# One scan step for both directions of an RWKV-7 scan: a shared PSUM bank, joint copies, four opening products together

## The chip, the cores and the metric

The kernel runs on one core of one Trainium2 chip. The metric is the device time of one execution in microseconds (us), smaller is better. Engines are called PE (TensorE, matrix products), PEld (its weight loads), DVE (VectorE), ACT (ScalarE), POOL (GpSimd) and SP (SyncE, which here only issues DMAs). PSUM is the memory that PE writes its products into, in banks of 2 KB for each of 128 partitions; SBUF is the on-chip memory that everything else works from.

## The reference, cut to what matters

The kernel computes one layer of a diffusion backbone over 1024 latent tokens of 1024 channels, with 256 context tokens in front. Three parallel branches are fed by one input projection: a neighbourhood attention, an RWKV-7 time mixing that runs in both directions, and a gated spatial mixing. Each branch is projected and gated, the sum is projected once more, and a SwiGLU feed-forward follows. The change touches the RWKV branch alone, whose core is a recurrence on one 64x64 state for each of 8 heads and 2 directions:

```python
def delta_scan(state0, inputs, emit):
    def step(S, inp):
        r_t, w_t, k_t, v_t, kk_t, a_t = inp
        s_kk = jnp.einsum('...vk,...k->...v', S, kk_t)
        S = (S * w_t[..., None, :] - s_kk[..., :, None] * (kk_t * a_t)[..., None, :]
             + v_t[..., :, None] * k_t[..., None, :])
        return S, (jnp.einsum('...vk,...k->...v', S, r_t) if emit else None)
    return lax.scan(step, state0, inputs)
```

It runs first over the 256 context tokens without output, and from there over the 1024 latent tokens with output. The backward direction runs over reversed time. The outputs of both directions are added, normalised per head and gated.

## The kernel before, in words

Stages in order of time: input scaling and the projections that the scan needs, the scan, the attention with the scan's readout beside it, the mixer (branch and output projections), and the feed-forward. Most wide products are split into a high and a low half (`hh`, `hl` and `wh`, `wl`) and made as three products of 128x512 each (lines 222 to 224, whose results are called `d` in the profile).

**The scan** (`rwkv_run`, line 561) works on chunks of 64 tokens. Within a chunk the recurrence is a triangular system, so a chunk costs a few products and one state update. Heads come in pairs; a job `m` is one head pair `j` and one block `i` of 256 tokens, that is four chunks `u`, for both directions. `L` lists 20 jobs, in the order of two head pairs in turn; block 0 is the context. A job needs three things:
- `prep` (line 625), once for each direction: loads, decays `E`, the products of the chunk's vectors into PSUM tiles `gr` (line 662), and their masked copies into `KKe`, `KKo` (three sets of buffers, line 647), `BB` and `G`.
- `invert` (line 691), once for both directions: `G` goes through DRAM, DVE solves small blocks (lines 704 to 709), the result comes back through DRAM, and 64x64 products (line 725) build the inverse `X`.
- `step` (line 744), once for each direction and chunk, 160 times in all. Here is what a step does, as the prediction follows it. Its *opening products* (752) multiply state and values `rv` by `KKe` and `KKo` into `sc[lo]` and `sc[hi]`, the two heads of the pair on partitions 0 to 63 and 64 to 127. DVE and ACT copy this right side to `rb` (755, 756). Two products with `X` (758) give the solution, which ACT and DVE copy, negated, to `ub` (759, 760). Six *closing products* (764, 767; in context blocks 771, 773) give new state and output in the same bank. DVE and ACT scale the new state into `rv` of the next chunk (777, 778), and ACT copies the output to `y` (782, twice). Each `matmul` of the program is two records of the trace.

`sc` has two PSUM banks (`bufs=2`), so the two directions' steps take turns on them: the next step of a direction takes the bank that its last one used. The framework keeps two engines off one bank at a time: DVE reads its half, then ACT reads the other. `rb` and `ub` are rings of four tiles with zeros outside the written blocks.

**What sets the order.** The program is traced in the order of the Python code, and the framework's scheduler then fixes every engine's order when the kernel is built, by that order and by its own cost estimates. Work traced late can be put into time that it believes idle. That is how 28 projections that are needed only after the scan (`filling`, line 542: queries for the attention and branch gates; `fill(4)` and `fill(24)` in `build`, traced after scan and attention) come to stand on PE between the products of the scan. They are called *fillers* here: 48 products of 128x512 each.

**Around a step.** `values` (584) loads the values of job `m+2` into `rv` by eight DMAs at SP, in four tiles of four chunks each. `y` goes to DRAM from ACT's queue (618), one DMA for each direction. The readout loads it again, one direction at a time (944, 945), as 4 KB rows with a chunk's token on the partitions.

Of the kernel before, what the change touches and what calls it, by code (L numbers as in the profile page):

```python
# [17 lines left out]
P = 128  # L18
# [18 lines left out]
LEAD, LAG, AHEAD = 2, 2, 5  # L37
NPP, NPT = 4, 3
SIDE = 16
NWR, NHT, NHS, NO4, NO2 = 3, 8, 2, 6, 4  # L40

PV = {}
# [16 lines left out]
class Kern:  # L59
# [501 lines left out]
    def rwkv_run(self):  # L561
        nc, a, c, rp, s = self.nc, self.a, self.c, self.rp, self.s
# [19 lines left out]
        rvs, Js = {}, {}  # L582

        def values(m):
            j, i = L[m]
            rv = rvs[m] = [[self.T([P, 4, 64], f"rv{d}{h}", 3) for h in range(2)] for d in range(2)]
            for d in range(2):
                if i == 0:
                    nc.gpsimd.memset(rv[d][0][0:64, 3 * d, :], 0.0)
                    nc.gpsimd.memset(rv[d][1][64:128, 3 * d, :], 0.0)  # L590
                V = s["vtok"][j]
                n0 = self.start(d, i)
                for h in range(2):
                    nc.sync.dma_start(rv[d][h][64 * (1 - h):64 * (1 - h) + 64, 0:4, :],
                                      bass.AP(V.tensor, V.offset + 64 * h + n0 * P, [[P, 64], [P * 64, 4], [1, 64]]))

        def prepare(m):
            j, i = L[m]
            G = self.T([P, 2, 4, 64], "G", 2)
            Js[m] = [self.prep(m, j, d, i, G[:, d]) for d in range(2)]  # L600
            self.invert(Js[m])

        self.filler = self.filling()
# [4 lines left out]
        for m, (j, i) in enumerate(L):  # L608
            if m + 2 < len(L):
                values(m + 2)  # L610
            y = [self.T([P, 2, P], f"y{d}", 2) for d in range(2)] if i else [None, None]
            for u in range(4):
                for d in range(2):
                    self.step(Js[m][d], d, i, u, rvs[m][d], rvs[m + 2][d] if i < 4 else None, y[d])
            if i:
                for d in range(2):
                    c0 = 4 * (i - 1) if d == 0 else 16 - 4 * i
                    nc.scalar.dma_start(s["Y"][d][j][:, 64 * c0:64 * c0 + 256], y[d].rearrange("p c v -> p (c v)"))
# [6 lines left out]
    def prep(self, m, j, d, i, G):  # L625
# [10 lines left out]
        E = self.T([P, 4, 65], "E", 6)  # L636
        nc.gpsimd.memset(E[:, :, 0:1], 1.0)
        nc.scalar.activation(E[:, :, 1:65], units(R(li)), AF.Exp, scale=-C05)
        le = self.T([P, 256], "le", 2)
# [7 lines left out]
        KKe, KKo = self.sets[(m % 3) * 2 + d]  # L647
# [9 lines left out]
        prev = None  # L657
        for u in range(4):
            re = (KKe[0:64, u, :].rearrange("p (x t) -> p x t", t=64)[:, 0:3:2, :] if lat else KKe[0:64, u, 0:64])
            for o, x, y in ((go, BK[64:128, u, :], KKo[64:128, u, 0:W]), (ge, BK[0:64, u, :], re)):  # L660
                with self.tc.issue_after(prev.ins) if prev is not None else nullcontext():
                    prev = nc.tensor.matmul(o[:, u, 0:W], x, y, start=True, stop=True)
# [4 lines left out]
        BB = self.T([P, 4, P], "BB", 6)  # L667
# [18 lines left out]
        for o, t in ((BB[0:64, :, 0:64], tr[0:64, :, 0:64]), (KKe[64:128, :, 64:128], tr[64:128, :, 0:64]),  # L686
                     (BB[64:128, :, 64:128], tr[0:64, :, 64:128]), (KKo[0:64, :, 128:192], tr[64:128, :, 64:128])):
            nc.scalar.activation(o, t, AF.Copy)
        return dict(KKe=KKe, KKo=KKo, G=G, BB=BB, E=E, n0=n0, lat=lat)

    def invert(self, jobs):
        nc, c = self.nc, self.c
# [48 lines left out]
        for d, J in enumerate(jobs):  # L741
            J["X"] = X[:, 4 * d:4 * d + 4]

    def step(self, J, d, i, u, rv, rvn, y):
        nc = self.nc
        lat, KKe, KKo, BB, X, E = J["lat"], J["KKe"], J["KKo"], J["BB"], J["X"], J["E"]
        v, w = (u, u + 1) if d == 0 else (3 - u, 2 - u)
        sc = self.ps.tile([P, 512], F32, name="sc", tag="sc", bufs=2)
        lo, hi = slice(0, 64), slice(64, 128)
        kk = (KKe[:, u], KKo[:, u])  # L750
        for z, q in enumerate((lo, hi)):
            nc.tensor.matmul(sc[q, 0:64], kk[z][:, 0:64], rv[z][:, v, :], start=True, stop=True)
        self.un += 1
        rb, ub = self.rb[self.un % 4], self.ub[self.un % 4]
        nc.vector.tensor_copy(rb[0:64, 0:64], sc[0:64, 0:64])
        nc.scalar.activation(rb[64:128, 64:128], sc[64:128, 0:64], AF.Copy)
        for q in (lo, hi):
            nc.tensor.matmul(sc[q, 64:128], X[:, u, :], rb[:, q], start=True, stop=True)
        nc.scalar.activation(ub[0:64, 0:64], sc[0:64, 64:128], AF.Copy, scale=-1.0)
        nc.vector.tensor_scalar(ub[64:128, 64:128], sc[64:128, 64:128], -1.0, None, ALU.mult)  # L760
        if lat:
            for z in range(2):
                for h, q in enumerate((lo, hi)):
                    nc.tensor.matmul(sc[q, 128 + 64 * z:192 + 64 * z], kk[z][:, 64 + 64 * h:128 + 64 * h], rv[z][:, v, :],
                                     start=(z == 0), stop=False)
            for q in (lo, hi):
                nc.tensor.matmul(sc[q, 128:256], BB[:, u, q], ub, start=False, stop=True)
            so = 192
        else:
            for z, q in enumerate((lo, hi)):  # L770
                nc.tensor.matmul(sc[q, 128:192], kk[z][:, 64 + 64 * z:128 + 64 * z], rv[z][:, v, :], start=True, stop=False)
            for q in (lo, hi):
                nc.tensor.matmul(sc[q, 128:192], BB[:, u, q], ub[:, q], start=False, stop=True)
            so = 128
        if not (i == 4 and u == 3):
            dst = (rv[0][:, w, :], rv[1][:, w, :]) if u < 3 else (rvn[0][:, 3 * d, :], rvn[1][:, 3 * d, :])
            nc.vector.tensor_scalar(dst[0][0:64], sc[0:64, 128:192], E[0:64, u, 64:65], None, ALU.mult)  # L777
            nc.scalar.activation(dst[1][64:128], sc[64:128, so:so + 64], AF.Copy, scale=E[64:128, u, 64:65])  # L778
        if lat:
            q = slice(64 * (v % 2), 64 * (v % 2) + 64)  # L780
            for z, p0, c0 in ((0, 64, 128), (1, 0, 192)):
                nc.scalar.activation(y[q, v // 2, 64 * z:64 * z + 64], sc[p0:p0 + 64, c0:c0 + 64], AF.Copy)


    def A(self, shape, tag, bufs, dt=F32):
# [149 lines left out]
    def readout(self):  # L935
        nc, a, s, c = self.nc, self.a, self.s, self.c
        for j in range(4):
# [4 lines left out]
            Y = self.X([P, 16, 64], "A4", 6)  # L942
            Y2 = self.X([P, 16, 64], "A4", 6)
            for y, d in ((Y, 0), (Y2, 1)):
                nc.sync.dma_start(y.rearrange("p c v -> p (c v)"), s["Y"][d][j])
# [515 lines left out]
```

## Time and profile before

| what | value |
|---|---|
| median of 3 runs | 2424.2 us (2419.29 to 2430.45) |
| the profiled execution, its own time | 2425.41 us |
| its span, first to last instruction | 2423.6 us |
| mean granted clock of PE | 0.974 |
| scan, from the first solution products to the last step | about 568 to 1155 us |
| attention, with readout | about 1160 to 1440 us |
| a stretch of fillers alone | within 1440 to 1500 us |
| mixer and feed-forward | from about 1500 us |

A profile row of a group reads: line, engine, operation, output<-inputs, shapes, count, then the time that the group keeps its engine busy, the mean of one in ns, and the idle time of the engine just before it with what ended it. A row of the windows view reads: start and end, length, then for PE, PEld, DVE, ACT, POOL the busy time and the count of instructions, and last PE's granted clock, the DMA engines' busy share and GB/s. Restricted to a tile, it counts the instructions that write or read that tile alone. A row of the timeline is start, length, engine, line, operation and tiles; "x4" merges four neighbours. Lengths of PE's rows overlap, because products are pipelined: what one costs is the distance from its start to the next start.

### The profile page before, as it was taken

How to read it: one execution, taken by the hardware profiler on the slowest of the kernel's cores; microseconds unless marked ns; L12 is line 12 of the kernel's file. 1: busy time of each engine (PE TensorE's matmuls, PEld its weight loads, DVE VectorE, ACT ScalarE, POOL GpSimd, SP SyncE). 2: the span in 40 equal slices, each digit the busy share in tenths (PEclk: the TensorE clock that was granted, in tenths of full speed). 3: DMA queues.
4: the chain of work that ended last, by engine and by line, in shares of the span. 5: the costliest groups of instructions: out<-in, count | busy, mean ns of one | idle time of the engine just before them, and what ended most of it. 6: DMA issues, size and time to landing. Idle time of an engine off the chain costs nothing. (4 is left out here: it accounts for less than half of the span.)

```text
span 2423.6 us, 40691 instructions
## 1 busy us (share of the span) xinstructions
PE 2288.6 (94%) x15352; PEld 1799.6 (74%) x15352; DVE 1557.5 (64%) x3290; ACT 948.3 (39%) x1985; POOL 684.2 (28%) x718
## 2 busy tenths in 40 slices
PE   6899999999999999989999999999799999999997
PEld 4778888776666766666777778778588888887886
DVE  8885446347777788774377833777665555555835
ACT  4432424233455445444355532232533333333421
POOL 6221213441121122111221330232433333425402
PEclk9999999999999999999999999999899999999999
DMA  7676444554344344432666564555132222237541
GB/s 248 213 235 164 142 137 150 173 146 116 91 100 110 96 118 111 101 71 60 186 183 172 178 216 163 168 196 161 61 105 79 79 81 85 88 138 269 170 161 53
DMA packets 276121, 337.53 MB, mean 139 GB/s; under 512 B 123314, under 2 KB 194226, under 8 KB 275924
## 3 DMA queue, kind: packets, MB, share of 16 engines
q1 hardware_dynamic: 208804, 240.91, 33.5%
q10 hardware_dynamic: 54608, 51.40, 7.1%
q0 software_dynamic: 12512, 42.62, 4.8%
q8 instruction: 121, 1.98, 0.3%
q14 instruction: 76, 0.62, 0.1%
HBM read 248.85 MB, written 85.99 MB: 138 GB/s over the span
## 5 line engine op out<-in xcount | busy, mean ns | idle before, releaser
L222 PE MATMUL d<-hh,wh 128*128 128x512 f32 x1056 | 431.4, 408 | 1.2 <-ACT stg L539 1.2
L224 PE MATMUL d<-hh,wl 128*128 128x512 f32 x1056 | 432.2, 409 | 0.0
L223 PE MATMUL d<-hl,wh 128*128 128x512 f32 x1056 | 431.5, 409 | 0.0
L224 PEld LDWEIGHTS d<-hh,wl 128*128 128x128 f32 x1056 | 201.5, 191 | 47.3 <-issue 4.4
L222 PEld LDWEIGHTS d<-hh,wh 128*128 128x128 f32 x1056 | 201.7, 191 | 45.1 <-issue 3.6
L223 PEld LDWEIGHTS d<-hl,wh 128*128 128x128 f32 x1056 | 201.5, 191 | 43.5 <-issue 2.3
L214 DVE TENSOR_TENSOR wl<-wr,wh 128x1024 fp32r<-128x1024 f32 x51 | 65.0, 1274 | 185.2 <-ACT wh L210 136.8
L210 ACT ACTIVATE wh<-wr 128x1024 fp32r<-128x1024 f32 x79 | 83.6, 1058 | 205.4 <-PE d L223 157.7
L214 POOL TENSOR_TENSOR wl<-wr,wh 128x256 fp32r<-128x256 f32 x112 | 87.2, 807 | 245.8 <-ACT wh L210 192.2
L239 DVE TENSOR_TENSOR o<-wr,o 128x1024 fp32r<-128x1024 f32 (+1 forms) x64 | 93.8, 1467 | 19.7 <-ACT o L236 19.2
L1022 PE MATMUL d<-dl,ah 128*128 128x512 f32 x252 | 98.3, 390 | 2.5 <-DVE dl L239 2.5
L906 PE MATMUL pv<-pT,V 128*64 128x128 f32 (+2 forms) x640 | 95.6, 287 | 4.5 <-ACT pT L894 3.0
L236 ACT ACTIVATE o<-wr 128x1024 fp32r<-128x1024 f32 (+1 forms) x64 | 59.2, 926 | 101.4 <-PE d L223 74.4
L1023 PE MATMUL d<-dh,al 128*128 128x512 f32 x252 | 98.1, 389 | 0.0
L1021 PE MATMUL d<-dh,ah 128*128 128x512 f32 x252 | 98.0, 389 | 0.0
L239 DVE TENSOR_TENSOR al<-ar,ah 128x512 fp32r<-128x512 f32 x42 | 42.1, 1020 | 75.1 <-ACT ah L236 75.1
L1016 POOL TENSOR_TENSOR wl<-wr,wh 128x1024 fp32r<-128x1024 f32 x16 | 42.7, 2671 | 167.9 <-DVE wr L1014 123.3
L778 ACT ACTIVATE rv<-sc,E 64x64 f32<-64x64 f32 x152 | 46.6, 308 | 108.4 <-DVE rv L777 90.2
L906 PEld LDWEIGHTS pv<-pT,V 128*64 128x64 f32 (+2 forms) x640 | 69.4, 139 | 24.4 <-issue 13.8
L1249 POOL TENSOR_TENSOR act<-act 128x512 f32<-128x512 f32 x22 | 28.7, 1306 | 194.3 <-issue 160.1
L707 DVE TENSOR_TENSOR dtmp<-gz,DD 64x15 f32<-64x15 f32 (+2 forms) x300 | 72.2, 241 | 11.4 <-POOL DD L703 3.7
L709 DVE TENSOR_TENSOR DD<-DD,dtmp 64x15 f32<-64x15 f32 (+2 forms) x300 | 73.7, 246 | 5.5
(403 smaller groups left out, 6019.4 us busy)
## 6 DMA issues: line engine op xcount, KB each, us to landing
wr<-wgu SPq DMA_DIRECT2D x45, 512.0 KB
dr<-wdn SPq DMA_DIRECT2D x42, 512.0 KB
wa<-wada SPq DMA_DIRECT2D x32, 512.0 KB
wr<-win SPq DMA_DIRECT2D x31, 512.0 KB
wr<-win ACTq DMA_DIRECT2D x28, 512.0 KB
s_gt<-stg ACTq DMA_DIRECT2D x48, 256.0 KB
wr<-wbr SPq DMA_DIRECT2D x24, 512.0 KB
g<-s_gt SPq DMA_DIRECT2D x48, 256.0 KB
```

The lines of the kernel that those rows point to most:

```text
L210: nc.scalar.activation(hi[:, :n], raw[:, :n], AF.Copy)
L214: (lo_eng or self.lo_eng).tensor_tensor(lo[:, q], raw[:, q], hi[:, q].bitcast(F32), ALU.subtract)
L222: nc.tensor.matmul(ps, w, xh, start=first and k == 0, stop=False)
L223: nc.tensor.matmul(ps, w, xl, start=False, stop=False)
L224: self.last = nc.tensor.matmul(ps, lo[:, P * k:P * k + P], xh, start=False, stop=last and k == n - 1)
L239: (lo_eng or nc.vector).tensor_tensor(lo, src, hi.bitcast(F32), ALU.subtract)
L707: nc.vector.tensor_tensor(t, z[:, q, q + 1:16].unsqueeze(2).to_broadcast([64, n, w]), Dm[:, q, 0:w].unsqueeze(1).to_broadcast([64, n, w]), ...
L709: nc.vector.tensor_tensor(Dm[:, q + 1:16, 0:w], Dm[:, q + 1:16, 0:w], t, ALU.add)
L906: nc.tensor.matmul(o, V[0:k, vt, 64 * e:64 * e + 64], pt[0:k, i, :], start=(i == 0), stop=(i == len(cols) - 1))
L1021: nc.tensor.matmul(ps, xh, wh, start=first, stop=False)
L1022: nc.tensor.matmul(ps, xh, wl, start=False, stop=False)
L1023: nc.tensor.matmul(ps, xl, wh, start=False, stop=last)
```

## The change

`step` serves both directions at once, so there are 80 of them.
- One bank `sc` of [128, 2, 256] holds both directions; still two banks, now used in turn by consecutive joint steps.
- `rb` and `ub` hold both directions ([128, 2, 128], rings of three). DVE copies the right side of both directions for head `lo` in one instruction, ACT for head `hi`; the same for the solution. The new state of head `lo` is one DVE product with a broadcast `E`; that of head `hi` stays two ACT instructions, one for each direction. The output is two ACT copies in place of four.
- `rv`, `y` and `E` are joint tiles; chunk `u` of the forward direction sits at index `u`, of the backward one at `7 - u`.
- The opening products are issued backward direction first, and the other three are tied behind the first one in PE's order.
- `y` now has a head on each half of the partitions, for all eight chunks. The readout therefore loads each direction's output with four DMAs of 64 partitions and 64-element runs in place of one of whole rows.

The number and shape of the products is the same. The core of the diff:

```diff
+NRB = 3
...
-        for i in range(4):
+        for i in range(NRB):
             for n, l in (("rb", self.rb), ("ub", self.ub)):
-                t = rp.tile([P, P], F32, name=f"{n}{i}")
+                t = rp.tile([P, 2, P], F32, name=f"{n}{i}")
...
-            rv = rvs[m] = [[self.T([P, 4, 64], f"rv{d}{h}", 3) for h in range(2)] for d in range(2)]
+            rv = rvs[m] = [self.T([P, 8, 64], f"rv{h}", 3) for h in range(2)]
...
+            E = self.T([P, 2, 4, 65], "E", 3)
+            Js[m] = [self.prep(m, j, d, i, G[:, d], E[:, d]) for d in range(2)]
...
-            y = [self.T([P, 2, P], f"y{d}", 2) for d in range(2)] if i else [None, None]
+            y = self.T([P, 8, 64], "y", 2) if i else None
             for u in range(4):
-                for d in range(2):
-                    self.step(Js[m][d], d, i, u, rvs[m][d], rvs[m + 2][d] if i < 4 else None, y[d])
+                self.step(Js[m], Es[m], i, u, rvs[m], rvs[m + 2] if i < 4 else None, y)
...
-    def step(self, J, d, i, u, rv, rvn, y):
+    def step(self, J, E, i, u, rv, rvn, y):
+        lat = i > 0
+        at = (u, 7 - u)
+        two = lambda p, q: slice(p, q + 1, q - p)
+        sc = self.ps.tile([P, 2, 256], F32, name="sc", tag="sc", bufs=2)
         self.un += 1
+        rb, ub = self.rb[self.un % NRB], self.ub[self.un % NRB]
+        prev = None
+        for d in (1, 0):
+            for z, q in ((1, hi), (0, lo)):
+                with self.tc.issue_after(prev.ins) if prev is not None else nullcontext():
+                    x = nc.tensor.matmul(sc[q, d, 0:64], J[d]["kk"][z][:, u, 0:64], rv[z][:, at[d], :], start=True, stop=True)
+                prev = prev or x
+        nc.vector.tensor_copy(rb[lo, :, 0:64], sc[lo, :, 0:64])
+        nc.scalar.activation(rb[hi, :, 64:128], sc[hi, :, 0:64], AF.Copy)
+        for d in range(2):
+            for q in (lo, hi):
+                nc.tensor.matmul(sc[q, d, 64:128], J[d]["X"][:, u, :], rb[:, d, q], start=True, stop=True)
+        nc.scalar.activation(ub[lo, :, 0:64], sc[lo, :, 64:128], AF.Copy, scale=-1.0)
+        nc.vector.tensor_scalar(ub[hi, :, 64:128], sc[hi, :, 64:128], -1.0, None, ALU.mult)
+        for d in range(2):
             for z in range(2):
                 for h, q in enumerate((lo, hi)):
+                    if lat or z == h:
+                        c0 = 128 + 64 * z * lat
+                        nc.tensor.matmul(sc[q, d, c0:c0 + 64], J[d]["kk"][z][:, u, 64 + 64 * h:128 + 64 * h], rv[z][:, at[d], :],
+                                         start=(z == 0 or not lat), stop=False)
             for q in (lo, hi):
+                o, x = (sc[q, d, 128:256], ub[:, d, :]) if lat else (sc[q, d, 128:192], ub[:, d, q])
+                nc.tensor.matmul(o, J[d]["BB"][:, u, q], x, start=False, stop=True)
+        so = 192 if lat else 128
         if not (i == 4 and u == 3):
+            o, w = (rv, two(u + 1, 6 - u)) if u < 3 else (rvn, two(0, 7))
+            nc.vector.tensor_tensor(o[0][lo, w, :], sc[lo, :, 128:192], E[lo, :, u, 64:65].to_broadcast([64, 2, 64]), ALU.mult)
+            for d in range(2):
+                nc.scalar.activation(o[1][hi, (w.start, w.stop - 1)[d], :], sc[hi, d, so:so + 64], AF.Copy, scale=E[hi, d, u, 64:65])
         if lat:
+            w = two(*at)
+            nc.scalar.activation(y[hi, w, :], sc[hi, :, 128:192], AF.Copy)
+            nc.scalar.activation(y[lo, w, :], sc[lo, :, 192:256], AF.Copy)
...
             for y, d in ((Y, 0), (Y2, 1)):
-                nc.sync.dma_start(y.rearrange("p c v -> p (c v)"), s["Y"][d][j])
+                for q in range(2):
+                    for h in range(2):
+                        nc.sync.dma_start(y[64 * q:64 * q + 64, h:16:2, :], s["Y"][d][j][64 - 64 * h:128 - 64 * h].rearrange(
+                            "p (n q v) -> p q n v", q=2, v=64)[:, q])
```

The removed body of the old `step` is in the listing above.

More of the change, by code (lines that the diff above doesn't have):

```diff
@@ L581, in rwkv_run @@
         L = [(2 * g + j, i) for g in range(2) for i in range(5) for j in range(2)]
-        rvs, Js = {}, {}
+        rvs, Js, Es = {}, {}, {}
         def values(m):
             j, i = L[m]
-            rv = rvs[m] = [[self.T([P, 4, 64], f"rv{d}{h}", 3) for h in range(2)] for d in range(2)]
+            rv = rvs[m] = [self.T([P, 8, 64], f"rv{h}", 3) for h in range(2)]
+            if i == 0:
+                for h in range(2):
+                    nc.gpsimd.memset(rv[h][64 * h:64 * h + 64, 0:8:7, :], 0.0)
+            V = s["vtok"][j]
             for d in range(2):
[L588 to L591, printed above, removed]
                 n0 = self.start(d, i)
                 for h in range(2):
-                    nc.sync.dma_start(rv[d][h][64 * (1 - h):64 * (1 - h) + 64, 0:4, :],
+                    nc.sync.dma_start(rv[h][64 * (1 - h):64 * (1 - h) + 64, 4 * d:4 * d + 4, :],
                                       bass.AP(V.tensor, V.offset + 64 * h + n0 * P, [[P, 64], [P * 64, 4], [1, 64]]))
@@ L599, in prepare @@
             G = self.T([P, 2, 4, 64], "G", 2)
-            Js[m] = [self.prep(m, j, d, i, G[:, d]) for d in range(2)]
+            E = self.T([P, 2, 4, 65], "E", 3)
+            Js[m] = [self.prep(m, j, d, i, G[:, d], E[:, d]) for d in range(2)]
+            Es[m] = E
             self.invert(Js[m])
@@ L610, in rwkv_run @@
                 values(m + 2)
-            y = [self.T([P, 2, P], f"y{d}", 2) for d in range(2)] if i else [None, None]
+            y = self.T([P, 8, 64], "y", 2) if i else None
             for u in range(4):
-                for d in range(2):
-                    self.step(Js[m][d], d, i, u, rvs[m][d], rvs[m + 2][d] if i < 4 else None, y[d])
[L615 to L618, printed above, removed]
+                self.step(Js[m], Es[m], i, u, rvs[m], rvs[m + 2] if i < 4 else None, y)
+            for d in range(2 if i else 0):
+                c0 = 4 * (i - 1) if d == 0 else 16 - 4 * i
+                nc.scalar.dma_start(s["Y"][d][j][:, 64 * c0:64 * c0 + 256], y[:, 4 * d:4 * d + 4, :].rearrange("p c v -> p (c v)"))
             if m + 2 < len(L):
@@ L623, in start, with prep @@
         return 0 if i == 0 else (CT + 256 * (i - 1) if d == 0 else NT - 256 * i)
-    def prep(self, m, j, d, i, G):
+    def prep(self, m, j, d, i, G, E):
         nc, c, s = self.nc, self.c, self.s
@@ L635, in prep @@
         R = rev if d else (lambda x: x)
-        E = self.T([P, 4, 65], "E", 6)
         nc.gpsimd.memset(E[:, :, 0:1], 1.0)
@@ L688, in prep @@
             nc.scalar.activation(o, t, AF.Copy)
-        return dict(KKe=KKe, KKo=KKo, G=G, BB=BB, E=E, n0=n0, lat=lat)
+        return dict(kk=(KKe, KKo), G=G, BB=BB)
     def invert(self, jobs):
@@ L742, in invert @@
             J["X"] = X[:, 4 * d:4 * d + 4]
-    def step(self, J, d, i, u, rv, rvn, y):
+    def step(self, J, E, i, u, rv, rvn, y):
         nc = self.nc
-        lat, KKe, KKo, BB, X, E = J["lat"], J["KKe"], J["KKo"], J["BB"], J["X"], J["E"]
-        v, w = (u, u + 1) if d == 0 else (3 - u, 2 - u)
-        sc = self.ps.tile([P, 512], F32, name="sc", tag="sc", bufs=2)
+        lat = i > 0
         lo, hi = slice(0, 64), slice(64, 128)
-        kk = (KKe[:, u], KKo[:, u])
-        for z, q in enumerate((lo, hi)):
-            nc.tensor.matmul(sc[q, 0:64], kk[z][:, 0:64], rv[z][:, v, :], start=True, stop=True)
+        at = (u, 7 - u)
+        two = lambda p, q: slice(p, q + 1, q - p)
+        sc = self.ps.tile([P, 2, 256], F32, name="sc", tag="sc", bufs=2)
@@ L753, in step @@
         self.un += 1
[L754 to L760, printed above, removed]
@@ L766, in step @@
             for q in (lo, hi):
[L767 to L774, printed above, removed]
+                o, x = (sc[q, d, 128:256], ub[:, d, :]) if lat else (sc[q, d, 128:192], ub[:, d, q])
@@ L779, in step @@
         if lat:
-            q = slice(64 * (v % 2), 64 * (v % 2) + 64)
-            for z, p0, c0 in ((0, 64, 128), (1, 0, 192)):
-                nc.scalar.activation(y[q, v // 2, 64 * z:64 * z + 64], sc[p0:p0 + 64, c0:c0 + 64], AF.Copy)
+            w = two(*at)
+            nc.scalar.activation(y[hi, w, :], sc[hi, :, 128:192], AF.Copy)
+            nc.scalar.activation(y[lo, w, :], sc[lo, :, 192:256], AF.Copy)
     def A(self, shape, tag, bufs, dt=F32):
@@ L944, in readout @@
             for y, d in ((Y, 0), (Y2, 1)):
-                nc.sync.dma_start(y.rearrange("p c v -> p (c v)"), s["Y"][d][j])
+                for q in range(2):
+                    for h in range(2):
+                        nc.sync.dma_start(y[64 * q:64 * q + 64, h:16:2, :], s["Y"][d][j][64 - 64 * h:128 - 64 * h].rearrange(
+                            "p (n q v) -> p q n v", q=2, v=64)[:, q])
             nc.vector.tensor_tensor(Y, Y, Y2, ALU.add)
```

6 lines of the change are left out of this document (removed).

## Prediction

> **What bounds the kernel now.** I read the page's first lines, then the windows view by stage.
>
> ```profile
> span 2423.6 us, 40691 instructions
> PE 2288.6 (94%) x15352; PEld 1799.6 (74%) x15352; DVE 1557.5 (64%) x3290; ACT 948.3 (39%) x1985; POOL 684.2 (28%) x718
> 568.00:1155.00 587.00, 550.68 (x6889) 395.71 (x6889) 437.43 (x1487) 282.83 (x994) 99.77 (x202) 0.96 0.39 95
> 1160.00:1440.00 280.00, 267.82 (x1627) 208.78 (x1626) 187.41 (x580) 138.78 (x258) 75.82 (x52) 0.98 0.62 184
> 1440.00:1500.00 60.00, 58.80 (x257) 47.75 (x256) 12.42 (x15) 14.28 (x19) 5.69 (x8) 1.00 0.51 176
> 1500.00:2423.00 923.00, 883.38 (x3867) 720.51 (x3865) 574.28 (x707) 300.79 (x396) 317.47 (x213) 0.98 0.39 128
> ```
>
> PE is busy in every stage: 94% of the scan, 96% of the attention and of all that follows, 98% of the stretch 1440 to 1500. So the time is PE's work plus PE's idle time. The scan is no exception, since fillers stand in its gaps, and a filler that finds no place there runs in the stretch from 1440 on, at its own price. A shorter scan is therefore worth nothing by itself. What counts is whether the same products cost PE less time, idle time included.
>
> A busy PE isn't a cheap PE, though, and the windows restricted to the filler results `d` show it (first row the scan, second a stretch of fillers alone, third the last job's steps):
>
> ```profile
> 568.00:1155.00 587.00, 239.24 (x695) 120.92 (x695) 0.00 (x0) 16.56 (x28) 0.96 0.39 95
> 1445.00:1480.00 35.00, 34.48 (x150) 27.93 (x150) 0.00 (x0) 3.93 (x7) 1.00 0.36 122
> 1133.00:1155.00 22.00, 14.47 (x39) 6.48 (x40) 0.00 (x0) 0.60 (x1) 1.00 0.13 43
> ```
>
> Alone, a filler product takes 34.48 / 150 = 0.23 us. In the scan one covers 239.24 / 695 = 0.34 us, in the last job's steps 14.47 / 39 = 0.37 us. The surplus in the scan, 695 x 0.11 = 76 us, is what PE pays for going back and forth between fillers and small products (the half-rate clock of a few windows, granted share 0.96, is in it as well).
>
> **What one visit costs.** A *visit* is an unbroken run of `sc` products on PE. PE's timeline in the last job, where little else runs, reads:
>
> ```profile
> 1140.00 0.34 PE L758 MATMUL sc<-rb,X 128*64 128x64 f32 x4
> 1140.27 0.51 PE L223 MATMUL d<-hl,wh 128*128 128x512 f32 x1
> 1140.61 0.40 PE L224 MATMUL d<-hh,wl 128*128 128x512 f32 x1
> 1140.93 0.34 PE L758 MATMUL sc<-rb,X 128*64 128x64 f32 x4
> 1141.20 0.49 PE L222 MATMUL d<-hh,wh 128*128 128x512 f32 x1
> 1141.62 0.34 PE L764 MATMUL sc<-rv,KKe 128*64 128x64 f32 x4
> 1142.23 0.49 PE L223 MATMUL d<-hl,wh 128*128 128x512 f32 x1
> ```
>
> From start to start, the four records of one direction's solution take 0.27 us, the filler after them 0.34, the filler before the next four 0.32. Against 0.23 the two edges cost 0.11 + 0.09 = 0.20 us a visit. Both directions in one run also occur in this trace, early in the scan (first pair) and at its end (second pair):
>
> ```profile
> 568.42 0.45 PE L758 MATMUL sc<-rb,X 128*64 128x64 f32 x8
> 568.80 0.37 PE L662 MATMUL gr<-KKo,BK 64*128 64x128 f32 x1
> ...
> 1152.26 0.34 PE L764 MATMUL sc<-rv,KKe 128*64 128x64 f32 x4
> 1152.99 0.39 PE L767 MATMUL sc<-ub,BB 128*64 128x128 f32 x4
> 1153.31 0.50 PE L222 MATMUL d<-hh,wh 128*128 128x512 f32 x1
> ```
>
> Eight records take 0.38 us where two visits of four take 0.54: 0.16 less. The closing products of both directions take 1153.31 - 1152.26 = 1.05 us, of one 1142.23 - 1141.62 = 0.61: 1.22 - 1.05 = 0.17 less. So a visit saved is worth 0.16 + 0.20 = 0.36 us.
>
> **How many visits go.** Before, a step has three groups of products (opening, solution, closing) for each direction, 160 x 3 = 480 groups. They don't make 480 visits: the scheduler often puts groups side by side. Going through PE's rows of the whole scan I count 325 visits, the first at 568.42 and the last at 1152.26 to 1153.31, both shown. After, a joint step has three groups, 80 x 3 = 240, all of the same number of products as before. The groups wait on one another through DVE and ACT, so within a job they can't join, and I take 240 visits. 325 - 240 = 85 visits x 0.36 us = **-31 us**.
>
> Bounds: if the scheduler lets fillers in between the products of a joint group, visits stay and this is 0. At the other end stands the last job: its 22.00 us hold four steps and 39 fillers worth 39 x 0.23 = 9.0 us, so a step of both directions costs PE 13.0 / 4 = 3.26 us. Joint, it would cost 0.38 + 0.38 + 1.05 + 3 x 0.20 = 2.41 us. Were all steps like that, it would be 0.85 x 80 = -68 us.
>
> **The waits.** PE's idle time in front of the three kinds of groups, the DVE and ACT work of a step, and the longest waits that touch it:
>
> ```profile
> L752 PE MATMUL sc<-rv,KKe 128*64 128x64 f32 x316 | 49.8, 242 | 12.3 <-ACT y L782 5.8 <-DVE KKo L649 5.6 <-ACT rv L778 0.8
> L758 PE MATMUL sc<-rb,X 128*64 128x64 f32 x640 | 54.3, 245 | 6.1 <-ACT rb L756 5.7
> L764 PE MATMUL sc<-rv,KKe 128*64 128x64 f32 x512 | 45.2, 249 | 7.2 <-DVE ub L760 6.8
> L755 DVE COPY rb<-sc 64x64 f32<-64x64 f32 x158 | 33.4, 213 | 23.7 <-PE sc L752 22.0
> L756 ACT ACTIVATE rb<-sc 64x64 f32<-64x64 f32 x158 | 34.0, 217 | 46.5 <-DVE rb L755 36.8 <-DVE DD L709 2.4 <-DVE dtmp L707 1.9
> L759 ACT ACTIVATE ub<-sc 64x64 f32<-64x64 f32 x160 | 33.7, 216 | 98.2 <-PE sc L758 86.4 <-PE sc L752 4.4 <-PE gr L665 2.0
> L760 DVE TENSOR_SCALAR ub<-sc 64x64 f32<-64x64 f32 x160 | 35.8, 227 | 23.1 <-ACT ub L759 18.5
> L777 DVE TENSOR_SCALAR rv<-sc,E 64x64 f32<-64x64 f32 x152 | 41.4, 274 | 26.9 <-PE sc L767 19.5 <-PE sc L752 3.3 <-PE sc L773 0.7
> L778 ACT ACTIVATE rv<-sc,E 64x64 f32<-64x64 f32 x152 | 46.6, 308 | 108.4 <-DVE rv L777 90.2 <-DVE dtmp L707 5.9 <-DVE DD L709 5.6
> L782 ACT ACTIVATE y<-sc 64x64 f32<-64x64 f32 x256 | 54.9, 215 | 8.4 <-PE sc L767 4.1 <-PE sc L752 1.3 <-ACT y L782 0.5
> L688 ACT ACTIVATE BB<-gr 64x256 f32<-64x256 f32 x70 | 26.3, 375 | 9.9 <-PE gr L665 8.2 <-DVE G L672 0.5
> L739 DVE TENSOR_TENSOR X<-ho,Dt 128x128 f32<-128x128 f32 x19 | 5.5, 289 | 9.7 <-PE ho L725 9.6
> POOL E L637 <- ACT rv L778: 143.4, 29, 14.4
> ```
>
> PE stands for 12.3 + 6.1 + 7.2 = 25.6 us in front of the scan's groups. 5.8 of it is the opening products waiting for the output copy: a direction's next step takes the bank that this copy still reads. With joint steps taking the two banks in turn, the next opening needs the other bank and the copy can follow it: **-6 us**. Late next is the state's last ACT copy, which the opening products needed anyway.
>
> The rest of the idle time I leave at 20 us. The links of a joint step are longer. DVE's copies of 64x128 lie between 0.21 (64x64) and 0.29 us (128x128 with two inputs), say 0.25; ACT's between 0.22 and 0.38 (64x256), a third of the way, 0.27; the state product about 0.29, then two ACT copies of 0.31. That makes (0.25 + 0.27) + (0.27 + 0.25) + (0.29 + 0.62) = 1.95 us of links a joint step, 156 us in all, against 0.21 + 0.22 + 0.22 + 0.23 + 0.27 + 0.31 = 1.46 us a step, 234 us in all, of which 25.6 us or 11% show as idle PE. The same share of 156 would be 17 us, close to the 20. Bounds: 0 idle (another -20), or the links bare (the slower rival).
>
> That two directions' products alternate in two banks now is what hides one direction's links behind the other's products. The Trainium skill, "Perfetto Trace Analysis", section Matmuls, says that independent groups should rotate through different PSUM banks so that emptying one overlaps the next group's products; it speaks against one bank for both directions, and by it alone the slower rival's 2472 would be the sum instead of 2388. The trace takes no side: it has fillers in the links as well (1140.27 and 1140.61, between the two directions' solutions).
>
> **At nothing.** DVE and ACT execute fewer instructions in a step (6 to 3 and, with output, 10 to 6). They are at 437 and 283 of 587 us, and PE, not they, ends the stage; if they did, DVE would give 160 x 0.71 - 80 x 0.79 = 50 us. The joint `E` and buffer sets are freed when both directions are done, not one after the other: POOL's long wait for `E` is this loop, and fillers cover it. The rings of three joint tiles reach further back than four single ones.
>
> The readout's loads:
>
> ```profile
> A<-s_Y SPq DMA_DIRECT2D x8, 512.0 KB
> L945 SPq DMA_DIRECT2D A<-s_Y x8: 327/421/543, 1179.5 to 1368.9; - x8
>   DMA A<-s_Y: 0.9, 1
> ```
>
> Eight issues become 32, 24 x 0.42 = 10 us more at SP over some 190 us, and 4 KB rows become 256-byte runs. Behind them in SP's queue are the attention's loads of keys, queries and bias, which are issued ahead. The sum `Y + Y2` waited 0.9 us once. I put it at 0; bare, it is +10.
>
> **The sum.** -31 - 6 = -37 us. The profiled execution took 2425.4 us (span 2423.6 and 1.8 around it), 1.2 over the median 2424.2. 2425.4 - 37 = **2388 us**.
>
> **Rivals.** *Bare links, slower.* With one chain where two alternated, PE has no scan product during the 156 us of links, only what fillers the scheduler put there by its own estimates. For: PE does stand today where those estimates are short (5.7 us for `rb`, 6.8 for `ub`). Against: 695 fillers are there to be placed, and a joint step leaves room for some eight. It decides from (31 + 26) / 156 = 37% bare: there the idle time eats the saved visits. At two thirds bare, which I take as its price, idle is 104 us: 2425.4 - 31 + (104 - 26) = 2472.
>
> *The saved time becomes idle, no change.* If the scan's length is set by the loop through `E` (a job's preparation waits for the steps of the job three before it, POOL's 143.4 us) and the built order holds no more fillers than before, PE idles where it was slow. The time stays at 2425 less the 6 us of the bank wait: 2419. For: the built order doesn't know PE's edge costs, so it won't add fillers for them. Against: PE is busy 94% in the scan, so there is little slack for the loop to rule.
>
> *It doesn't do what it says.* The tie of the opening products is an order, not a closeness; if fillers stand between, visits don't fall and the time is again about 2419.
>
> *Larger gain.* All steps save as in the last job: 2425.4 - 68 - 6 = 2351.
>
> **How the numbers follow.** Forecast 0.52, larger gain 0.09, no change by the loop 0.14, by scattered products 0.07, bare links 0.18. A measurement of this kernel can tell about 0.5%, 12 us, from no change. The forecast's upper edge and both cases of no change make "same" 0.24, so faster is 0.58 and slower 0.18. The range goes from the larger gain, 2351, to 2440: that takes in the forecast with its bounds, no change, and bare links up to about 45%; it leaves out some 0.2. The faster cases' own range is 2351 to 2412.
>
> **What would show it.** Right: visits near 240, a filler product in the scan below 0.31 us, no idle time of the opening products on the output copy, scan products' idle time at about 20 us. Wrong: idle time in front of the solution or closing products above 50 us in all (bare links), PE busy below 90% in the scan (the loop), visits above 300 (scattered). A longer attention stage would mean that the readout's loads count.

## The result and the profile after

The changed kernel took 2395.7 us in the median of its runs (2386.5 to 2401.9), the kernel before 2421.7 us (2414.4 to 2430.5) in the runs beside it: a ratio of 0.9886, 95% interval 0.9858 to 0.9913. It is faster by 26 us. The forecast was 2388 us, 37 us below the kernel before; 26 of the 37 came. The profiled executions are 30.7 us apart: 2425.4 before, 2394.7 after.

The page of the changed kernel opens with span and busy times (busy us, share, number of instructions):

```profile
span 2392.9 us, 40066 instructions
PE 2253.3 (94%) x15352; PEld 1790.2 (75%) x15352; DVE 1531.1 (64%) x3054; ACT 895.3 (37%) x1697; POOL 683.8 (29%) x708
```

PE's products are the same 15352 and cost 35.3 us less. The windows by stage (stretch, its length, busy time of PE, PEld, DVE, ACT, POOL, granted clock, DMA share, GB/s) say where:

```profile
563.00:1120.00 557.00, 515.95 (x6893) 385.77 (x6890) 408.27 (x1253) 228.25 (x706) 99.12 (x200) 0.95 0.41 99
1160.00:1440.00 280.00, 265.79 (x1595) 209.13 (x1593) 184.24 (x547) 133.64 (x246) 75.09 (x52) 0.97 0.63 177
1440.00:1500.00 60.00, 59.73 (x261) 48.51 (x261) 35.07 (x47) 16.94 (x21) 0.00 (x0) 1.00 0.68 222
1500.00:2392.00 892.00, 851.89 (x3723) 693.19 (x3721) 546.51 (x674) 291.85 (x385) 318.90 (x213) 0.98 0.37 124
```

The scan takes 557 us in place of 587 with as many products (6893 and 6889). What follows it is about as long as before, 2392.9 - 1120 = 1273 us against 2423.6 - 1155 = 1269. The windows of the scan restricted to a tile (PE, PEld, DVE, ACT; first `d`, then `sc`):

```profile
563.00:1120.00 557.00, 218.51 (x687) 122.25 (x688) 0.00 (x0) 16.54 (x28) 0.95 0.41 99
563.00:1120.00 557.00, 160.21 (x3064) 121.41 (x3064) 66.58 (x235) 109.62 (x439) 0.95 0.41 99
```

The same for `sc` in the kernel before:

```profile
568.00:1155.00 587.00, 185.40 (x3064) 133.20 (x3064) 109.36 (x470) 162.27 (x726) 0.96 0.39 95
```

So 3064 `sc` products cover 160 us where they covered 185, and a filler 218.51 / 687 = 0.318 us where it covered 0.344. PE's timeline of a joint step shows both (start, duration, engine, line, product, records):

```profile
774.06 0.40 PE L224 MATMUL d<-hl,wh 128*128 128x512 f32 x1
774.39 0.45 PE L763 MATMUL sc<-rb,X 128*64 128x64 f32 x8
774.77 0.51 PE L225 MATMUL d<-hh,wl 128*128 128x512 f32 x1
...
776.27 0.40 PE L225 MATMUL d<-hh,wl 128*128 128x512 f32 x1
776.60 0.34 PE L771 MATMUL sc<-rv,KKe 128*64 128x64 f32 x4
...
777.33 0.39 PE L775 MATMUL sc<-ub,BB 128*64 128x128 f32 x4
777.65 0.50 PE L223 MATMUL d<-hh,wh 128*128 128x512 f32 x1
```

Both directions' solution is one run of 0.38 us (774.39 to 774.77), their closing products one of 1.05 us (776.60 to 777.65), and only the fillers next to a run are long: 0.33 us from start to start ahead of each, against 0.23 alone. All three agree with the forecast's numbers (0.38, 1.05, and 0.32 to 0.34 for a filler at an edge).

PE's groups of the scan by line and form (busy, mean ns, idle time in front of it and what ended that), with the copies of DVE and ACT:

```profile
L771 PE MATMUL sc<-rv,KKe 128*64 128x64 f32 x576 | 50.6, 238 | 4.4 <-DVE ub L765 4.2
L662 PE MATMUL gr<-KKo,BK 64*128 64x128 f32 x246 | 48.7, 316 | 19.0 <-DVE KKo L649 18.4 <-POOL KKo L653 0.4
L763 PE MATMUL sc<-rb,X 128*64 128x64 f32 x640 | 37.9, 243 | 3.9 <-ACT rb L760 3.5
L757 PE MATMUL sc<-rv,KKo 128*64 128x64 f32 x316 | 33.0, 234 | 6.9 <-ACT rv L781 6.5
...
L765 DVE TENSOR_SCALAR ub<-sc 64x128 f32<-64x128 f32 x80 | 23.5, 294 | 19.8 <-ACT ub L764 17.8
L759 DVE COPY rb<-sc 64x128 f32<-64x128 f32 x79 | 21.7, 279 | 21.4 <-PE sc L757 20.6
L779 DVE TENSOR_TENSOR rv<-sc,E 64x128 f32<-64x128 f32 x76 | 21.4, 281 | 20.6 <-PE sc L775 18.9
L764 ACT ACTIVATE ub<-sc 64x128 f32<-64x128 f32 x80 | 21.6, 271 | 70.3 <-PE sc L763 66.5 <-DVE G L672 0.9 <-PE sc L757 0.9
L760 ACT ACTIVATE rb<-sc 64x128 f32<-64x128 f32 x79 | 21.1, 272 | 55.7 <-DVE rb L759 46.7 <-DVE DD L709 4.9 <-POOL bi L798 1.9
```

The scan's groups now wait 6.9 + 3.9 + 4.4 = 15.2 us (25.6 before), and none for the output copy. A new wait stands at the Gram products (`gr`, the products of a chunk's vectors in `prep`): 19.0 us in front of them. The same group before:

```profile
L662 PE MATMUL gr<-KKo,BK 64*128 64x128 f32 x246 | 48.9, 307 | 2.1 <-DVE KKo L649 1.9
```

**The account.** I went through PE's rows of the scan in both traces. Each product is charged from its start to the next start, less the idle time named there; a filler's *surplus* is what it costs above 0.229 us; a visit is an unbroken run of `sc` products; `ho` are the products that build the inverse. In us:

| | visits | fillers | `sc` time | filler surplus | idle before `sc` / `gr` / `ho` |
|---|---|---|---|---|---|
| before | 325 | 694 | 162.7 | 63.7 | 25.9 / 2.1 / 8.3 |
| after | 222 | 687 | 145.1 | 50.1 | 15.3 / 19.0 / 6.8 |

103 visits fewer, -17.6 in the products and -13.6 in the fillers: -31.2 us, 0.30 a visit. Idle time: -10.6 at `sc`, +16.9 at `gr`, -1.5 at `ho`. One more number serves below, the *price of the scan*: its length (counted from 505 us, ahead of all its work) less 0.229 us for each filler in it. It is 458.8 before and 427.2 after. What is left of the span then, *the rest*, is 2423.6 - 505 - 458.8 = 1459.8 before and 2392.9 - 505 - 427.2 = 1460.7 after: unchanged. The gain is in the scan's price. A second profile of the changed kernel (the run again, below) has a price of 422.4 us and a rest of 1461.6, so some 5 us of a price are scatter between executions.

### The profile page after: what moved, and what is told of

Read it like the earlier page. It is cut to its first block, busy times and chain, and to the rows that moved or that the text cites. A ratio compares the mean times of both kernels' runs of the same rounds, so it can differ in the third digit from the quotient of the medians.

```text
span 2392.9 us, 40066 instructions
## 1 busy us (share of the span) xinstructions
PE 2253.3 (94%) x15352; PEld 1790.2 (75%) x15352; DVE 1531.1 (64%) x3054; ACT 895.3 (37%) x1697; POOL 683.8 (29%) x708
## 4 chain that ended last, share of the span: by engine, by line
PE 68%; DVE 16%; DMA 5%; issue 4%; ACT 4%; POOL 3%; SPq 0%; ACTq 0%; DVEq 0%; POOLq 0%
PE d L225 13%; PE d L223 13%; PE d L224 13%; PE ho L725 3%; PE pv L909 3%; PE d L1028 3%; PE d L1029 3%; PE d L1027 3%; PE gr L662 2%; PE pt L895 2%; DVE w L243 1%; DVE junk L243 1%; PE sc L771 1%; DVE DD L709 1%; DVE dtmp L707 1%
## 5 line engine op out<-in xcount | busy, mean ns | idle before, releaser
L781 ACT ACTIVATE rv<-sc,E 64x64 f32<-64x64 f32 x152 | 38.9, 303 | 123.1 <-DVE rv L779 112.8
L662 PE MATMUL gr<-KKo,BK 64*128 64x128 f32 (+1 forms) x320 | 61.5, 313 | 24.3 <-DVE KKo L649 21.2
```

## The experiments

Ratios are to the kernel before, run on the same chip. The changed kernel was run again beside the second set: 0.9882 (0.9848 to 0.9915), 2392.1 us. The rest moves between about 1454 and 1468 us among kernels that don't touch it, as the built order differs; a difference of less than some 8 us between two edited kernels is not put down to the edit. Two kernels lie above that: the one with longer links (1475.5 us) and the one with one bank (1504.3), whose scans end last of all, at 1176 and 1192 us.

### One part of the change alone, or undone

**Four buffers for the joint `E`.**

```diff
-            E = self.T([P, 2, 4, 65], "E", 3)
+            E = self.T([P, 2, 4, 65], "E", 4)
```

> The changed kernel with four joint E tiles in place of three, so that a job's E no longer waits for the steps three jobs before it; the KK sets still do. Main theory (the saved PE visits are worth about 31 us, and 17 us of that went into a new wait in front of the gram products, because E and the KK sets come free for both directions at once, at the end of the joint steps): idle time in front of gram products falls from 19 us to below 8, time 5 to 12 us below the changed kernel, 31 to 38 below the kernel before. Rival (the gram products wait for the KK sets or for DVE's queue, not for E): idle stays above 14 us and the time within 4 us of the changed kernel.

Measured: 0.9856 (0.9833 to 0.9879), 2391.1 us. Three groups of its scan and POOL's wait for `E` (us in all, times, longest):

```profile
L662 PE MATMUL gr<-KKo,BK 64*128 64x128 f32 x246 | 46.6, 310 | 2.3 <-POOL KKo L653 2.1
L763 PE MATMUL sc<-rb,X 128*64 128x64 f32 x640 | 37.6, 241 | 6.7 <-DVE X L739 2.8 <-ACT rb L760 2.3 <-DVE dtmp L707 1.2
L757 PE MATMUL sc<-rv,KKo 128*64 128x64 f32 x316 | 34.2, 238 | 14.0 <-ACT rv L781 10.8 <-DVE dtmp L707 2.8
```
```profile
POOL E L637 <- ACT rv L781: 30.1, 4, 12.0
```

In the changed kernel that wait reads:

```profile
POOL E L637 <- ACT rv L781: 141.1, 11, 19.7
```

Before the change its 143.4 us were 29 waits of 4.9 us on average; joint, they are 11 of 12.8. With a fourth buffer the Gram products' wait is gone (19.0 to 2.3 us), so the joint `E` was its cause. But the opening products now wait 14.0 us where they waited 6.9, and idle time at `sc` is 27.1 us in all where it was 15.3. The time isn't the 5 to 12 us lower that was expected: the kernel without the tie (below), which has the changed kernel's visits and ran on the same chip, took 2391.8 us. The idle time moved.

**Each joint copy as two.** The products stay joined; each copy of DVE and ACT is split by direction.

```diff
-        nc.vector.tensor_copy(rb[lo, :, 0:64], sc[lo, :, 0:64])
+        for d in range(2):
+            nc.vector.tensor_copy(rb[lo, d, 0:64], sc[lo, d, 0:64])
```

and so for `rb` of `hi`, `ub`, the state of `lo` and `y`.

> The joint step with its products as in the changed kernel, but every DVE and ACT copy made once for each direction again (6 and 10 in a step with output, as before). Main theory (the gain is PE's fewer visits): visits stay near 222, scan products' idle time grows with the links (0.98 us x 80 = 78 us longer, 10 to 15% of it bare, 8 to 12 us), and the time stays 12 to 20 us below the kernel before. Rival one (the gain is the smaller load of DVE and ACT): the time is back within 5 us of the kernel before.

Measured: 0.9978 (0.9958 to 0.9997), 2418.4 us, only 5 below before. The windows of its scan, whole and of tile `d`:

```profile
565.00:1168.00 603.00, 553.93 (x7028) 415.29 (x7025) 443.39 (x1488) 263.75 (x1000) 109.19 (x212) 0.94 0.39 97
565.00:1168.00 603.00, 256.06 (x826) 149.05 (x827) 0.00 (x0) 20.14 (x34) 0.94 0.39 97
```

Visits stay at 229, so the merging is intact, and with it the saving in PE's products: `sc` time is 146.6 us and the filler surplus 54.8. Yet its price of the scan is 441.1 us, 14 above the changed kernel's. The saving goes into idle time, 27.4 us at `sc` and 15.4 at `gr`, more than before the change (25.9 and 2.1). The rest is 8 longer, no more than built orders differ. The scan is 46 us longer and holds 139 fillers more. The joint copies are no free by-product: without them most of the gain is lost. Splitting makes the links longer and gives DVE and ACT more to do, and this kernel doesn't separate the two.

**Without the tie of the four opening products.**

```diff
-                with self.tc.issue_after(prev.ins) if prev is not None else nullcontext():
+                if True:
                     x = nc.tensor.matmul(...)
```

> The changed kernel without the tie of the opening products. Main theory: the four have their inputs together, so the scheduler puts them together anyway or splits some; for each visit above 222 about 0.3 us is lost. If visits stay below 235 the time is within 5 us of the changed kernel; if the backward and forward pairs come apart, 80 more visits and 20 to 28 us, that is the whole gain. Rival one (DVE and ACT load) expects no change in either case.

Measured: 0.9873 (0.9852 to 0.9894), 2391.8 us, with 222 visits. The tie does nothing here; the scheduler issues the four together without it.

**One bank for consecutive steps.**

```diff
-        sc = self.ps.tile([P, 2, 256], F32, name="sc", tag="sc", bufs=2)
+        sc = self.ps.tile([P, 2, 256], F32, name="sc", tag="sc", bufs=1)
```

> The changed kernel with one PSUM bank for the joint steps, so that the opening products wait for the output copies of the step before, as they did before the change. Main theory: visits as in the changed kernel, idle time in front of the opening products up by 6 to 15 us, time 6 to 15 us above the changed kernel, still below the kernel before. Rival two (the gain is the bank that is free for the next step): all of the gain is lost, the time is within 5 us of the kernel before or above it.

Measured: 1.0124 (1.0104 to 1.0145), 2454.4 us: slower than the kernel before. Its windows: the scan, its fillers, and the stretch behind it.

```profile
563.00:1193.00 630.00, 580.69 (x7124) 429.96 (x7122) 425.54 (x1253) 238.93 (x721) 111.98 (x218) 0.95 0.39 96
563.00:1193.00 630.00, 282.24 (x924) 163.82 (x925) 0.00 (x0) 22.42 (x38) 0.95 0.39 96
1192.00:1500.00 308.00, 276.61 (x1607) 217.75 (x1602) 196.78 (x583) 139.71 (x259) 68.33 (x46) 0.92 0.61 166
```

In the changed kernel the stretch from the scan's end to the first branch projection reads:

```profile
1119.00:1445.00 326.00, 311.37 (x1818) 246.01 (x1818) 195.29 (x581) 148.56 (x271) 83.69 (x64) 0.97 0.64 179
```

And the groups of the scan with one bank:

```profile
L771 PE MATMUL sc<-rv,KKe 128*64 128x64 f32 x576 | 52.9, 245 | 13.9 <-DVE ub L765 13.9
L763 PE MATMUL sc<-rb,X 128*64 128x64 f32 x640 | 37.0, 237 | 14.3 <-ACT rb L760 14.2
L757 PE MATMUL sc<-rv,KKo 128*64 128x64 f32 x316 | 36.6, 241 | 2.2 <-ACT y L785 1.3
```

The expected wait for the output copy hardly shows in front of the opening products (1.3 us). The price of the scan is 445.8 us, 19 above the changed kernel's: idle time at the links (30.4 us in all) and 251 visits. The larger part is in the rest, 2455.1 - 505 - 445.8 = 1504.3 us, 44 more. The order spreads the longer scan over 924 fillers in place of 687, and then they run out: the last of these fillers ends at 1337 us, the last product of the attention at 1472. In the changed kernel the attention ends first, at 1397, with fillers up to 1445. PE idles 308.00 - 276.61 = 31.4 us in that stretch, in the changed kernel's 326.00 - 311.37 = 14.6. The clock is also lower there, 0.92 against 0.97, and why isn't shown. Some 14 of the 44 us come behind the first branch projection, which starts at 1493 us here and at 1445 in the changed kernel (961.9 us to the end against 947.8); they stay unexplained too.

**The readout's loads as before the change.** This leaves out the reordering of the scan's output that the new loads do.

```diff
-                for q in range(2):
-                    for h in range(2):
-                        nc.sync.dma_start(y[64 * q:64 * q + 64, h:16:2, :], ...)
+                nc.sync.dma_start(y.rearrange("p c v -> p (c v)"), s["Y"][d][j])
```

> The changed kernel with the readout's loads as before the change, eight whole tiles in place of 32 parts. The output's rows are then read in another order than they were written, so this leaves out the reordering of the scan's output. The prediction put the new loads at nothing: time within 4 us of the changed kernel. Rival (the issues at SP delay the attention's loads): 6 to 10 us below it.

Measured: 0.9884 (0.986 to 0.9907), 2398.1 us. The 32 small loads cost nothing that can be measured.

### What a change of kind on PE costs

Two kernels put one product with the identity between the two directions' closing products of each step, into columns that are no longer read. In the first it has 128 columns, like a filler; in the control 64, like the products around it.

```diff
+            if d == 0:
+                nc.tensor.matmul(sc[:, 0, 0:64], self.c["ident"][:, 0:128], rb[:, 0, 0:64], start=True, stop=True)
```
```diff
+            if d == 0:
+                nc.tensor.matmul(sc[lo, 0, 0:64], self.c["ident"][:, 0:64], rb[:, 0, 0:64], start=True, stop=True)
```

> The changed kernel with one product of 128 columns of weights (identity, 64 columns of data) between the closing products of the two directions; its result is used by nobody, nothing is left out. It breaks that visit by a change of the array's shape, 80 times, and puts in no wait. Main theory (a break costs 0.36 us, merging loss and edges): with the product's own 0.05 to 0.1 us, 28 to 37 us above the changed kernel. Rival (fewer visits are worth nothing by themselves, the gain is in the waits): at most 10 us above it, as the next kernel.

> The control of the one before: the product in the same place has 64 columns of weights like its neighbours, so the array's shape doesn't change. Both theories expect its own time alone, 80 x 0.05 to 0.1 us, 4 to 8 us above the changed kernel.

Measured: 1.0044 (1.002 to 1.0069), 2431.2 us with the wide product; 0.995 (0.9927 to 0.9972), 2409.3 us with the narrow one. PE's timeline of the first around a break:

```profile
801.94 0.39 PE L775 MATMUL sc<-ub,BB 128*64 128x128 f32 x4
802.26 0.43 PE L777 MATMUL sc<-rb,c_ident 128*128 128x64 f32 x2
802.63 0.34 PE L771 MATMUL sc<-rv,KKe 128*64 128x64 f32 x4
```

The break takes 802.63 - 802.26 = 0.37 us. The windows of the scan restricted to `sc`, wide product first:

```profile
563.00:1147.00 584.00, 200.57 (x3224) 144.74 (x3224) 66.58 (x235) 109.92 (x439) 0.94 0.38 95
563.00:1136.00 573.00, 169.47 (x3224) 131.01 (x3224) 66.32 (x235) 109.89 (x439) 0.94 0.40 97
```

Charged as in the account, `sc` time is 185.1 us with the wide product and 154.2 with the narrow one: (185.1 - 154.2) / 80 = 0.39 us for each change there and back, visits being equal (223 each). In it is what the wide product takes longer by itself; its weight loads last 189 ns a record against 137. The two kernels are 0.0094 or 23 us apart, less than 80 x 0.39 = 31: PE idles 29.0 us at `sc`, `gr` and `ho` with the wide product and 45.6 with the narrow one. (The profiled executions are 4.7 us apart, the wide kernel's being the fastest of its 12.) So a change of kind there and back costs about what the prediction put on a visit, 0.36 us, with no filler, no wait and no copy added. The control was dearer than I expected, some 16 us over the changed kernel; 154.2 - 145.1 = 9.1 of that is `sc` time, what the rest is stays open.

The Trainium skill, "TensorEngine Tiling (Array Packing)", section Key Properties, states that a change of tiling mode drains the TensorE. The 0.39 us agree with it; the traces show the time and not what the engine does in it, and the page has no price.

### Load or length of the links

Six 64x64 copies are added to each step, three on DVE and three on ACT. In the first kernel they touch nothing of the scan. In the second they rewrite `rb`, `ub` and the new state in place, so that the next product waits for them.

```diff
+        for _ in range(3):
+            nc.vector.tensor_copy(self.dv[1][lo], self.dv[0][lo])
+            nc.scalar.activation(self.da[1][lo], self.da[0][lo], AF.Copy)
```
```diff
+        nc.vector.tensor_copy(rb[lo, 0, 0:64], rb[lo, 0, 0:64])
+        nc.scalar.activation(rb[hi, 0, 64:128], rb[hi, 0, 64:128], AF.Copy)
...
+        nc.scalar.activation(ub[lo, 0, 0:64], ub[lo, 0, 0:64], AF.Copy)
+        nc.vector.tensor_copy(ub[hi, 0, 64:128], ub[hi, 0, 64:128])
...
+            nc.vector.tensor_copy(o[0][lo, w.start, :], o[0][lo, w.start, :])
+            nc.scalar.activation(o[1][hi, w.start, :], o[1][hi, w.start, :], AF.Copy)
```

> The changed kernel with six small copies more for each joint step that nobody waits for (three of 64x64 on DVE, three on ACT, from and to a tile of their own): the work of DVE and ACT is as great again as with split copies, the links are as short as in the changed kernel. It leaves nothing of the computation out. Links theory (splitting the copies lost 22 us because the links between PE's products got longer): at most 6 us above the changed kernel. Load theory (it lost them because DVE and ACT had more to do): 15 to 22 us above it.

> The changed kernel with the same six small copies as in the run with more load (three of 64x64 on DVE, three on ACT), but this time in the links: each writes a part of the right side, the solution or the state onto itself before the next products may use it. DVE's and ACT's load is that of the run with more load, the links are about 3 x 0.2 us longer for each joint step, 48 us in all, against 78 us with split copies, which lost 22. Links theory: 9 to 18 us above the changed kernel, a later end of the scan. If only the number of PSUM copies mattered, or the built order: within 5 us of it.

Measured beside the links: 0.9857 (0.9831 to 0.9884), 2389.9 us, nothing lost. But nothing holds these copies to their step, and the built order has all of them early. The rows give count, shortest, median and longest duration in ns, first and last start (the count at the end is of a sample):

```profile
L791 DVE COPY dv<-dv x240: 176/186/757, 512.2 to 712.4; 64x64 f32<-64x64 f32 x120
L792 ACT ACTIVATE da<-da x240: 238/256/259, 514.3 to 762.0; 64x64 f32<-64x64 f32 x120
```

The scan of this kernel:

```profile
563.00:1123.00 560.00, 515.61 (x6991) 388.09 (x6991) 429.92 (x1419) 277.36 (x920) 99.84 (x200) 0.95 0.40 100
```

In sum DVE and ACT are nearly as busy as before the change (430 and 277 us against 437 and 283), and nothing is lost. So the sum of their work is not where the gain comes from. What the same load would cost if it were spread over all steps, this kernel doesn't show, since from 762 us on it runs with the changed kernel's load.

Measured in the links: 1.0024 (1.0009 to 1.004), 2431.0 us, 34 us over the changed kernel by the ratios, twice what was expected. Here the copies do stand in every step. The scan, whole and tile `d`:

```profile
563.00:1177.00 614.00, 576.36 (x7094) 420.93 (x7094) 458.51 (x1501) 282.18 (x950) 107.19 (x209) 0.95 0.38 95
563.00:1177.00 614.00, 266.61 (x804) 142.66 (x804) 0.00 (x0) 20.05 (x34) 0.95 0.38 95
```

PE's idle time at `sc` hardly grows (17.6 us against 15.3). What grows is the number of visits, from 222 to 294: the joint groups fall apart. In the changed kernel 70 visits hold the eight records of a joint solution; here 25 do, while 40 hold two records and 36 six. Only one direction is rewritten, so the other one's products are free first; that this is the reason is argued, not shown. `sc` time and filler surplus are 162.0 + 66.3 us, 33 more than 145.1 + 50.1, for 72 visits: 0.46 each, with the surplus of 117 fillers more in it. The rest is 15 us longer as well. So this kernel undoes the saving of the change another way round, and it says little of what a longer link costs by itself. Why the split copies lose time is not settled by these two.

### Towards a faster version

**The state of head `hi` on DVE**, one product with a broadcast in place of two ACT instructions; and that with four buffers for `E`.

```diff
-            for d in range(2):
-                nc.scalar.activation(o[1][hi, (w.start, w.stop - 1)[d], :], sc[hi, d, so:so + 64], AF.Copy, scale=E[hi, d, u, 64:65])
+            nc.vector.tensor_tensor(o[1][hi, w, :], sc[hi, :, so:so + 64], E[hi, :, u, 64:65].to_broadcast([64, 2, 64]), ALU.mult)
```

> The changed kernel with the second head's state too as one DVE product for both directions, in place of two ACT copies: the last link is 0.28 + 0.28 us where it was 0.28 + 0.51, DVE has 21 us more to do and ACT 46 less. Links theory: scan ends 10 to 25 us earlier, time 2 to 8 us below the changed kernel. Load theory with DVE as the fuller engine: same or up to 10 us slower.

> Both state products on DVE, and four joint E tiles. If the two edits' gains add, 42 to 50 us below the kernel before; if PE's idle time only moves from the gram products to the scan's products, as four E tiles alone did, the same as the state on DVE alone, 38 to 42 below.

Measured: 0.9833 (0.9808 to 0.9858), 2385.3 us, for the first, and 0.9916 (0.9886 to 0.9946), 2402.0 us, for both. The first has the lowest time of all kernels here, 0.0049 below the changed kernel on the same chip (the intervals just overlap), but not by what was expected: its scan doesn't end earlier (1119 us) and its price is 421.8 us, against 422.4 of the changed kernel profiled beside it. Its profiled span is shorter in the rest, where nothing was edited. With a fourth `E` the scan's price goes up, to 432.2. I take neither as an effect of the edit that is understood.

## Why the prediction was right, and where it wasn't

*PE's work plus PE's idle time sets the time.* Held: PE is busy 515.95 / 557.00 = 93% in the scan, and the gain is in what its products cost. The added load on DVE and ACT, which cost nothing where it ran, fits this.

*A visit saved is worth 0.36 us; 85 go; -31 us.* The sum held by luck, as two errors cancel: 103 went, at 0.30 us. The price of one change of kind, measured by itself, is 0.39 us. The working took every visit to have a filler on both sides, and PE's rows show otherwise: of the 206 edges that went, 139 were to a filler (387 before, 248 after), 62 to a Gram product and 5 to `ho`. In the products a visit saved 17.6 / 103 = 0.17 us, in the fillers an edge saved 13.6 / 139 = 0.10 us, which are the forecast's 0.16 and 0.09 to 0.11. Its unit prices were right, and 1.35 edges with a filler go with each visit instead of two. The count fell below the forecast's 240, which took joint groups not to join further: of the 222 visits 72 are of solutions, 61 of openings, 83 of closings (some of these split in two) and 6 of several kinds, and 15 of those of openings hold the groups of two steps side by side.

*The output copy's wait, -6 us, and the rest of the idle time at 20.* The wait went. Idle time at `sc` fell by 10.6 us to 15.3, 4.6 us more than forecast. The durations taken for the longer copies, 0.25 and 0.27 us, were 0.28 to 0.29 and 0.27.

*The joint `E` and buffer sets at nothing, since fillers cover POOL's wait.* This is the step that failed. The wait for `E` comes less often and lasts longer, the Gram products behind it come late, and PE stands 16.9 us longer in front of them. The four-buffer kernel shows the cause of this wait. It doesn't show that the 17 us can be had back, as most of that idle time came up again at `sc`. -31.2 - 10.6 + 16.9 - 1.5 is -26.4 for the terms in the table; with smaller groups and the scan's margins the price fell by 31.6, and the profiled executions are 30.7 apart instead of 37.

*The tie, the readout's loads and the fewer instructions at nothing.* Held, each by a kernel of its own; for the instructions only as far as a load that ran early can test it.

*A shorter scan is worth nothing by itself.* It fits the changed kernel, whose fillers last beyond the attention and whose rest is unchanged. It is not a rule: with one bank the longer scan used them up, and a scan priced 19 us higher cost 58 (1.0124 - 0.9886 of 2424.1). The prediction's bound of 6 us on the bank wait was the price of the wait alone; it missed what a later scan does to the fillers.

*Bare links, the slower rival.* Fell: 15 us of idle time, not 104. The Trainium skill, "Perfetto Trace Analysis", section Matmuls, has the rule of different banks for independent groups, by which 2472 would have come out; for the two directions it did not decide, as they are faster joined in one bank. No kernel here joins their products and copies with a bank for each. As to consecutive steps the one-bank kernel agrees with it: both banks are needed. *Saved time becomes idle* fell in the large, as the scan became 30 us shorter, but its mechanism, the loop through `E`, is the one that took the 17 us. *Scattered opening products* fell with 222 visits.

Of the marks set beforehand, one was missed narrowly: a filler in the scan costs 0.318 us, not below 0.31.

Open: why the split copies lose time (longer links or more work), why the kernel with the state on DVE is faster, why one with a fourth `E` besides is not, and the clock behind the one-bank scan.

## What to carry to other kernels

When PE is busy all the time, count how often it changes between kinds of products and price a change from start to start, by the products on both edges too; merging groups then saves time with not one product fewer. Merge the copies between them as well, and look at which buffers are now freed together: whoever waits for them may wait longer, as POOL did for `E` here. Check that the background work that covers the chain outlasts the chain, since with one bank a scan 19 us dearer cost 58 once it had run out.

## What the runs showed of the hardware

A product of 128 columns between products of 64 costs 0.39 us more than one of 64 columns there (185.1 and 154.2 us of `sc` time, 80 such places), and a filler beside such a change 0.33 to 0.35 us from start to start in place of 0.23. A copy from PSUM of twice the width takes far less than twice as long at this size: 64x64 took 213 to 227 ns before, 64x128 took 271 to 294 after, so one copy for both directions saves a third of the time of two.
